# Expert 7's first layer cut into parts of 12, 2 and 2 blocks, TensorE's rounds of two blocks, and w2 of expert 6 in one load

## The chip, the cores and the metric

The kernel runs on one core of a Trainium2 chip. The metric is the device time of that core in microseconds (us). Before the change three runs gave 180.59, 180.69 and 180.82 us; the median is 180.69 us.

## What is computed

Eight experts, each a two-layer perceptron on its own 256 tokens:

```python
# x (8, 256, 512), w1 (8, 512, 2048), w2 (8, 2048, 512), b1 (8, 2048), b2 (8, 512), all float32
h = np.matmul(x, w1) + b1[:, np.newaxis, :]
h = np.maximum(h, 0)
return (np.matmul(h, w2) + b2[:, np.newaxis, :]).astype(np.float32)
```

The weights are read as float32 (4 MB each of w1 and w2 per expert, 64 MB in all) and converted to float16 while they are loaded, so that 2 MB per matrix arrive on the chip. The output is 4 MB of float32.

## The kernel before

Names: E = 8 experts, T = 256 tokens, `nJ` = 16 blocks of 128 hidden columns, `LAG` = 3, `NW` = 3 buffers each for w1 and w2, `NPH` = 4 banks of PSUM for first-layer results, `QJ` = 8 blocks, `nQ` = 2 halves of a second layer. In the text, l1(e) and l2(e) are the first and second layer of expert e, and w1(e), w2(e) the loads of its weights.

**TensorE** (`run_tensor`) runs one loop over the steps 0 to 10, written as a loop of the engine (`Fori`), not unrolled. Step s does l1(s), if s < 8, and then l2(s - 3), if s >= 3. l1 is an inner loop of four rounds of four blocks (L278); a block is four matmuls (L288) into one bank of `ph`. Every two blocks it waits on `ph_free` until ScalarE has emptied earlier banks (L282). Ahead of each pair of matmuls stands an instruction that computes their addresses (`ahead`, L262). l2 first puts the bias into `po` with two matmuls (L303); then an inner loop of two halves (L311), each of which waits on `w2_in` (L313) and runs 16 matmuls (L318). `po` has two buffers, used by even and odd experts. At the end of a second layer TensorE waits until the other buffer of `po` has been emptied (L336, L337), and for `ph_free` to reach a count that says that a whole further expert's hidden blocks are there (L338). Steps 8 to 10 hold only l2(5), l2(6) and l2(7).

**ScalarE** (`run_scalar`) takes blocks in order: bias, ReLU and conversion of each block of l1 from `ph` into `hT` (`relu`, L106), sixteen in a step, and after them the copy of that step's finished second layer from `po` (`evict`, L118). For experts 6 and 7 VectorE copies one half and ScalarE the other.

**VectorE** (`run_vector`) transposes x of experts 2 to 7 (L222) and makes its halves of the last two copies.

**GpSimd** (`run_gpsimd`) issues the weight loads on one queue, in a fixed order: w1(e) waits until l1(e - 3) is finished (L162), w2(e) until l2(e - 3) is finished (L167), since each takes over that expert's buffer. `CUT` splits w2(6) into two loads of 8 blocks and w2(7) into two of 11 and 5 blocks, each with a semaphore of its own. Once the first part of w2(7) has landed, GpSimd issues the stores of the outputs of experts 4 and 5 (1024 KB) and of experts 0 to 3 (2048 KB) (L183 to L188).

**SyncE** (`run_sync`) waits for each load in turn and passes the news on to TensorE as a count (L145 for w1, L151 for w2, two counts for each w2). After the first part of w2(7) it waits for the copy of expert 6 and stores that expert's output (512 KB, L155); after the loop it stores expert 7's (512 KB, L389). These two stores go on SyncE's own DMA queue.

At the start x of experts 0 and 1 is transposed by TensorE through the identity (L372), into the banks `ph[2]` and `ph[3]`, and ScalarE copies each result into `xT` (L373); then all engines meet, and the order written out by hand begins.

Of the kernel before, what the change touches and what calls it, by code (L numbers as in the profile page):

```python
# [10 lines left out]
def kernel(  # L11
# [22 lines left out]
    NW = 3  # L34
    NX = 4
    NH = LAG + 1
    NPH = 4

    GROUPS = {0: 4, 4: 2}
    GROUP_OF = {f + i: (f, n) for f, n in GROUPS.items() for i in range(n)}  # L40
    FIRST = {0: 1, 1: 1, 2: 2, 4: 4}
    X_OF = {f + i: (f, n, i) for f, n in FIRST.items() for i in range(n)}
    CUT = {E - 2: nJ // 2, E - 1: 11 * nJ // 16}
    nQ = 2
    QJ = nJ // nQ
    ENDS = nTB * nQ
# [1 line left out]
    def sb(name, shape, dt=fp16):  # L48
# [15 lines left out]
    steps = hT[:, NH - 1, 0 : B * B // T, :].rearrange("p a (n c) -> p (a n) c", c=B)  # L64
    steps_turned = hT[:, NH - 1, B * B // T : 2 * B * B // T, :].rearrange(
        "p a (n c) -> p (a n) c", c=B)
    ph = [nc.alloc_psum_tensor(f"ph{i}", [P, 512], fp32).ap() for i in range(NPH)]
    po = nc.alloc_psum_tensor("po", [P, 2, nTB, 512], fp32).ap()

    def sem(name):  # L70
# [10 lines left out]
    ph_full = sem("ph_full")  # L81
    ph_free = sem("ph_free")
# [74 lines left out]
    def run_gpsimd():  # L157
        g = nc.gpsimd

        def load_w1(e):  # L160
            if e >= NW:
                g.wait_ge(ph_full, nJ * (e - NW + 1))  # L162
            g.dma_start(out=w1_sb[:, e % NW], in_=w1_of(e)).then_inc(s_w1[e % NW], 16)  # L163

        def load_w2(e):
            if e >= NW:
                g.wait_ge(po_full, ENDS * (e - NW + 1))  # L167
            src = w2[e].rearrange("(p j) h -> p j h", j=nJ)
            cuts = (0, CUT[e], nJ) if e in CUT else (0, nJ)
            for h, (lo, hi) in enumerate(zip(cuts, cuts[1:])):  # L170
                g.dma_start(  # L171
                    out=w2_sb[:, e % NW, lo:hi], in_=src[:, lo:hi]).then_inc(s_w2[e, h], 16)

        for step in range(1, E + LAG):
            if step < E:
                if step == 4:
                    g.dma_start(out=x16[step], in_=x_of(step)).then_inc(s_x, 16)
                load_w1(step)
            if step == NW - 1:
                tc.wait_critical_data_deps()  # L180
            if step >= LAG:
                load_w2(step - LAG)
        g.wait_ge(s_w2[E - 1, 0], 16)  # L183
        for first in sorted(GROUPS, reverse=True):
            done = 1 + first + GROUPS[first]
            g.wait_ge(po_free_a, done)
            g.dma_start(out=out_of(first, GROUPS[first]), in_=grouped[first]).then_inc(  # L187
                s_out[first], 16)  # L188
    def run_scalar():
        a = nc.scalar  # L190
        a.sem_inc(ph_free, NPH)
        a.sem_inc(po_free_a, 1)
        a.sem_inc(po_free_d, 1 + len(GROUP_OF))
        a.sem_inc(xT_full, 2)  # L194
        a.copy(out=x16[2], in_=x32[2]).then_inc(cast, 1)  # L195
        for step in range(E + LAG):
            if step < E:
                for j in range(nJ):
                    a.wait_ge(ph_full, nJ * step + j + 1)
                    relu(step, j).then_inc(ph_free, 1)  # L200
# [36 lines left out]

    def run_tensor():
        t = nc.tensor
        mult, mod, least = (getattr(mybir.AluOpType, n) for n in ("mult", "python_mod", "min"))  # L240
# [4 lines left out]
        names = ("due", "w1_at", "x_at", "due2", "w2_at", "h_at", "o_at", "b_at", "next_e", "all_h", "next_s")  # L245
        due, w1_at, x_at, due2, w2_at, h_at, o_at, b_at, next_e, all_h, next_s = (
            t.alloc_register(n) for n in names)
        t.reg_mov(x_at, 0)
        for r in (w1_at, due2, w2_at, h_at, o_at, b_at, next_e):
            t.reg_add(r, x_at, 0)  # L250
        t.reg_add(due, x_at, 2)
        t.reg_add(next_s, x_at, 1)

        def val(r, top, low=0):
            return t.snap(r, min_val=low, max_val=top)

        def turn_over(r, by, size):
            t.reg_add(r, r, by)
            t.reg_alu(r, r, size, mod)
# [6 lines left out]
                "p (q j) -> p q j", j=nJ)[:, :, 0]  # L266

        with t.Fori(0, E + LAG) as s:
            with t.If(s < E):
                turn = val(next_s, E, 1)  # L270
                t.wait_ge(w1_in, turn)
                t.wait_ge(xT_full, turn)
                t.reg_add(next_s, next_s, 1)
                x_e = val(x_at, (NX - 1) * nKC * T)
                x_cols = [xT_f[:, bass.ds(x_e + kc * T, T)] for kc in range(nKC)]
                ahead(*x_cols[0:2])
                ahead(*x_cols[2:4])
                with t.Fori(0, nJ // NPH):  # L278
                    w1_j = val(w1_at, (NW - 1) * nKC * M + nJ - NPH)
                    for i in range(NPH):  # L280
                        if i % 2 == 0:
                            t.wait_ge(ph_free, val(due, E * nJ, 1))  # L282
                        for kc in range(nKC):
                            if kc % 2 == 0:
                                ahead(w1_cols(w1_j, i, kc), w1_cols(w1_j, i, kc + 1), weights=True)
                            if i % 2 == 1 and kc == nKC - 1:
                                t.reg_add(due, due, 2)
                            ins = t.matmul(  # L288
                                out=ph[i][:, 0:T],
                                lhsT=w1_cols(w1_j, i, kc),  # L290
                                rhs=x_cols[kc],
                                start=(kc == 0),
                                stop=(kc == nKC - 1),
                            )
                        ins.then_inc(ph_full, 1)
                    t.reg_add(w1_at, w1_at, NPH)
                turn_over(w1_at, nKC * M - nJ, NW * nKC * M)
                turn_over(x_at, nKC * T, NX * nKC * T)
            with t.If(s >= LAG):
                o = val(o_at, nTB * 512)  # L300
                b_e = val(b_at, (E - 1) * H)
                for tb in range(nTB):
                    t.matmul(  # L303
                        out=po_f[:, bass.ds(o + tb * 512, H)],
                        lhsT=ones1,
                        rhs=b2_sb[0:1, bass.ds(b_e, H)],
                        start=True,
                        stop=False,
                        skip_group_check=True,
                    )  # L310
                with t.Fori(0, nQ):  # L311
                    t.reg_add(due2, due2, 1)
                    t.wait_ge(w2_in, val(due2, nQ * E, 1))  # L313
                    w_e = val(w2_at, (NW * nJ - QJ) * H)
                    h_e = val(h_at, (NH * nJ - QJ) * T)
                    for tb in range(nTB):
                        for j in range(QJ):
                            ins = t.matmul(  # L318
                                out=po_f[:, bass.ds(o + tb * 512, H)],
                                lhsT=hT_f[:, bass.ds(h_e + (j * T + tb * P), P)],  # L320
                                rhs=w2_f[:, bass.ds(w_e + j * H, H)],
                                start=False,
                                stop=(j == QJ - 1),
                                skip_group_check=True,
                            )
                        ins.then_inc(po_full, 1)
                    turn_over(w2_at, QJ * H, NW * nJ * H)
                    turn_over(h_at, QJ * T, NH * nJ * T)
                turn_over(o_at, nTB * 512, 2 * nTB * 512)
                t.reg_add(b_at, b_at, H)  # L330
                t.reg_add(next_e, next_e, 1)
                t.reg_alu(all_h, next_e, nJ, mult)
                t.reg_add(all_h, all_h, nJ + NPH)
                t.reg_alu(all_h, all_h, E * nJ + NPH, least)
                done, turned = val(next_e, E, 1), val(all_h, E * nJ + NPH, 1)
                t.wait_ge(po_free_a, done)  # L336
                t.wait_ge(po_free_d, done)  # L337
                t.wait_ge(ph_free, turned)  # L338

    def first_loads():  # L340
        for to, rows in (
# [85 lines left out]
```

## Time and profile before

| what | value |
|---|---|
| median of three runs | 180.69 us |
| the profiled execution | 180.67 us, of which the span of the trace is 178.9 us |
| TensorE matmuls busy | 130.8 us (73%) |
| ScalarE busy | 86.2 us (48%) |
| VectorE busy | 37.7 us (21%) |
| moved by DMA | 40.98 MB at a mean of 229 GB/s, counted at the destination |
| read from memory / written to it | 71.39 MB / 4.19 MB |
| GpSimd's DMA queue (q0), SyncE's (q1) | 95.2% and 4.5% of 16 engines' span |

Times in the trace count from the start of the span. A row of the timeline gives the start, the length, the engine, the line, the operation and how many instructions were merged; in brackets stands the idle time before it and what ended that. "Landing" is the time from the issue of a transfer until its semaphore says that all of it has arrived. GpSimd's queue hands transfers to the 16 DMA engines in the order of issue. The share of DMA time over a short window can read above 1 because a packet is counted where it starts or overlaps.

### The profile page before, as it was taken

The page shows a single profiled execution, that of the slowest core. Times are in us where ns is not written, and L with a number is a line of the kernel's source. Part 1 is how long each engine was busy: PE and PEld are TensorE (multiplying, and loading weights), DVE is VectorE, ACT ScalarE, POOL GpSimd, SP SyncE. Part 2 cuts the span into 40 slices and gives each one's busy share as a digit, 9 for nine tenths or more (in the row PEclk, how much of TensorE's full clock was granted, in tenths as well). Part 3 has the DMA queues.
Part 4 walks back from the last instruction along what each step waited for, and adds up shares of the span by engine and source line. Part 5 has one row for each costly group of instructions (what it writes and reads, how often), then busy time and mean ns, then how long its engine had stood idle before and what let it go on. Part 6 is the DMA issues. An engine that isn't in the chain of part 4 may idle for free.

```text
span 178.9 us, 2880 instructions
## 1 busy us (share of the span) xinstructions
PE 130.8 (73%) x800; PEld 87.1 (49%) x800; DVE 37.7 (21%) x39; ACT 86.2 (48%) x160; POOL 13.4 (7%) x30
## 2 busy tenths in 40 slices
PE   0002299596969996999949993899389997997950
PEld 0002178585858742794338642764178543442410
DVE  0074099500000299992000000000000000001010
ACT  3302847585877803892099408970578303131010
POOL 7100000302020001001000001000200002000200
PEclk9999999999999999699999999999969999999995
DMA  5999989999999999998999999999899899999996
GB/s 215 265 255 277 233 183 231 234 205 207 234 209 202 234 212 198 234 231 183 231 234 201 209 234 205 205 234 220 191 234 231 187 227 205 214 213 212 335 440 256
DMA packets 3825, 40.98 MB, mean 229 GB/s; under 512 B 448, under 2 KB 464, under 8 KB 1136
## 3 DMA queue, kind: packets, MB, share of 16 engines
q0 software_dynamic: 3056, 37.76, 95.2%
q1 hardware_dynamic: 768, 3.21, 4.5%
q14 instruction: 1, 0.01, 0.0%
HBM read 71.39 MB, written 4.19 MB: 422 GB/s over the span
## 4 chain that ended last, share of the span: by engine, by line
DMA 62%; PE 20%; DVE 6%; ACT 4%; issue 3%; SPq 1%; ACTq 0%
DMA w1sb<-in_w_dram 43%; PE ph L288 12%; DMA outg<-in_x_dram 10%; DMA w2sb<-in_w_dram 10%; PE po L318 8%; DVE xTsb L222 6%; ACT hTsb L106 3%; ACT x L195 1%; SPq L347 1%; PE po L303 0%; ACT pair L118 0%; ACTq L422 0%; SPq L145 0%; SPq L151 0%; ACTq L194 0%
## 5 line engine op out<-in xcount | busy, mean ns | idle before, releaser
L288 PE MATMUL ph<-xTsb,w1sb 128*128 x512 | 68.1, 293 | 21.7 <-SPq L145 10.4
L288 PEld LDWEIGHTS ph<-xTsb,w1sb 128*128 x512 | 59.0, 148 | 31.9 <-issue 29.0
L106 ACT ACTIVATE hTsb<-ph,b1T 128x256 f16<-128x256 f32 x128 | 56.8, 474 | 15.4 <-PE ph L288 14.9
L318 PE MATMUL po<-w2sb,hTsb 128*128 x256 | 56.6, 379 | 2.3 <-SPq L151 2.3
L118 ACT COPY outg<-po 32x1024 f32<-32x1024 f32 (+1 forms) x20 | 20.1, 1005 | 43.3 <-PE po L318 43.2
L318 PEld LDWEIGHTS po<-w2sb,hTsb 128*128 x256 | 25.0, 98 | 32.8 <-issue 5.0
L222 DVE STREAM_TRANSPOSE xTsb<-x 32x512 f16<-32x512 f16 (+1 forms) x32 | 31.0, 970 | 35.0 <-DMA x<-in_x_dram 27.7
L118 DVE COPY pair<-po 128x512 f32<-128x512 f32 x2 | 1.4, 691 | 88.4 <-PE po L318 88.4
L372 PE MATMUL ph<-ident,x 128*128 128x128 f16 x16 | 1.9, 313 | 16.6 <-ACT ident L363 16.6
L171 POOL DMA_DIRECT2D w2sb<-in_w_dram x10 | 5.3, 534 | 70.7 <-PE po L318 70.7
L372 PEld LDWEIGHTS <-x 128*128 128x128 f16 x16 | 1.6, 148 | 16.6 <-ACT ident L363 16.6
L163 POOL DMA_DIRECT2D w1sb<-in_w_dram x7 | 3.7, 535 | 64.6 <-PE ph L288 64.4
L118 ACT COPY pair<-po 128x512 f32<-128x512 f32 x2 | 1.2, 585 | 13.8 <-PE po L318 13.8
L375 DVE STREAM_TRANSPOSE b1T<-b1rows 32x512 f32<-32x512 f32 x4 | 4.1, 1023 | 10.2 <-DMA b1rows<-in_b_dram 10.1
L303 PE MATMUL po<-b2sb,ones 1*128 x16 | 4.8, 379 | 0.9 <-issue 0.7
L363 ACT COPY ident<-hTsb 32x32 f16<-32x32 f16 x4 | 1.0, 240 | 9.2 <-DVE hTsb L360 9.1
L365 ACT CAST x<-pair 128x1024 f16<-128x1024 f32 x2 | 2.1, 1044 | 2.3 <-DMA pair<-in_x_dram 2.3
L303 PEld LDWEIGHTS po<-b2sb,ones 1*128 1x128 f16 x16 | 1.4, 91 | 3.5 <-issue 3.3
L373 ACT COPY xTsb<-ph 128x1024 f16<-128x1024 f16 x2 | 1.9, 1015 | 1.1 <-PE ph L372 1.1
L187 POOL DMA_DIRECT2D out_dram<-outg x2 | 1.1, 536 | 16.7 <-DMA w2sb<-in_w_dram 16.7
L195 ACT CAST x<-outg 128x2048 f16<-128x2048 f32 x1 | 1.9, 1900 | 0.8 <-DMA outg<-in_x_dram 0.8
L365 ACT ACT_TABLE_LOAD x1 | 1.3, 1283 | 0.7 <-PEq L411 0.7
(12 smaller groups left out, 5.0 us busy)
## 6 DMA issues: line engine op xcount, KB each, us to landing
w1sb<-in_w_dram POOLq DMA_DIRECT2D x8, 2048.0 KB, 30.6
w2sb<-in_w_dram POOLq DMA_DIRECT2D x6, 2048.0 KB, 43.8
w2sb<-in_w_dram POOLq DMA_DIRECT2D x2, 1024.0 KB, 28.4
out_dram<-outg POOLq DMA_DIRECT2D x1, 2048.0 KB, 10.9
w2sb<-in_w_dram POOLq DMA_DIRECT2D x1, 1408.0 KB, 17.5
pair<-in_x_dram SPq DMA_DIRECT2D x2, 512.0 KB, 3.8
outg<-in_x_dram SPq DMA_DIRECT2D x1, 1024.0 KB, 17.8
x<-in_x_dram POOLq DMA_DIRECT2D x1, 1024.0 KB, 27.7
```

The costliest lines, as they stand in the source:

```text
L106: return nc.scalar.activation(out=to, in_=columns, func=relu_of, bias=b1T[:, at : at + 1], scale=1.0)
L118: return copy(out=t.rearrange("p (tb s) h -> p tb s h", s=split)[at : at + rows, lo:hi, k, :], in_=po[k * rows : (k + 1) * rows, e % 2, lo ...
L163: g.dma_start(out=w1_sb[:, e % NW], in_=w1_of(e)).then_inc(s_w1[e % NW], 16)
L171: g.dma_start(out=w2_sb[:, e % NW, lo:hi], in_=src[:, lo:hi]).then_inc(s_w2[e, h], 16)
L195: a.copy(out=x16[2], in_=x32[2]).then_inc(cast, 1)
L222: ins = v.transpose(out=to[b * B : (b + 1) * B, :, :, half * B : (half + 1) * B], in_=src.rearrange("p r (i kc) -> p kc r i", kc=nKC))
L288: ins = t.matmul(out=ph[i][:, 0:T], lhsT=w1_cols(w1_j, i, kc), rhs=x_cols[kc], start=(kc == 0), stop=(kc == nKC - 1),)
L303: t.matmul(out=po_f[:, bass.ds(o + tb * 512, H)], lhsT=ones1, rhs=b2_sb[0:1, bass.ds(b_e, H)], start=True, stop=False, skip_group_check=True,)
L318: ins = t.matmul(out=po_f[:, bass.ds(o + tb * 512, H)], lhsT=hT_f[:, bass.ds(h_e + (j * T + tb * P), P)], rhs=w2_f[:, bass.ds(w_e + j * H, ...
L365: a.copy(out=x16[e], in_=x32[e])
L372: t.transpose(out=to[:, kc, r, :], in_=rows[:, kc, :], identity=ident)
L375: v.transpose(out=b1T[b * B : (b + 1) * B, nB - 1 - b : nB - 1 - b + nJ * B], in_=b1_rows.rearrange("r (i j) -> r j i", j=nJ))
```

## The change

- l1(7) is cut. `LAST = (6, 1, 1)` gives its rounds in steps 7, 8 and 9: 12 blocks ahead of l2(4), 2 blocks between l2(4) and l2(5), and 2 blocks between l2(5) and l2(6). The number of rounds left out of a step is held in a packed register (`skipped`) from which each step takes three bits as the first index of its inner loop.
- A round of l1 has two blocks in place of four, for all experts. The bank of `ph` is now computed from a register (`p_at`), so the four banks are one tensor `ph_all`. For expert 7 the pointers into w1 and x are not turned over between the parts.
- ScalarE takes 12 blocks of expert 7 in step 7, and the other 4 in step 8, ahead of the copy of expert 5.
- The wait for hidden blocks at the end of a second layer (L338) goes, with the three register operations that computed its count.
- w2(6) is one load of 2048 KB with one semaphore in place of two of 1024 KB.

```diff
+    ROUNDS = nJ // 2
+    LAST = (6, 1, 1)
+    SKIPPED = [0] * (E - 1) + [ROUNDS - n for n in LAST]
...
-    CUT = {E - 2: nJ // 2, E - 1: 11 * nJ // 16}
+    CUT = {E - 1: 11 * nJ // 16}
...
-    ph = [nc.alloc_psum_tensor(f"ph{i}", [P, 512], fp32).ap() for i in range(NPH)]
+    ph_all = nc.alloc_psum_tensor("ph", [P, NPH, 512], fp32).ap()
+    ph = [ph_all[:, i] for i in range(NPH)]
...
+    def columns_at(step):
+
+        if step < E - 1:
+            return range(nJ)
+        return {E - 1: range(2 * LAST[0]), E: range(2 * LAST[0], nJ)}.get(step, ())
+
     def run_scalar():
...
         for step in range(E + LAG):
-            if step < E:
-                for j in range(nJ):
-                    a.wait_ge(ph_full, nJ * step + j + 1)
-                    relu(step, j).then_inc(ph_free, 1)
+            for j in columns_at(step):
+                e = min(step, E - 1)
+                a.wait_ge(ph_full, nJ * e + j + 1)
+                relu(e, j).then_inc(ph_free, 1)
...
+        t.reg_add(skipped, x_at, sum(n << 3 * step for step, n in enumerate(SKIPPED)))
...
         with t.Fori(0, E + LAG) as s:
-            with t.If(s < E):
+            with t.If(s < len(SKIPPED)):
                 turn = val(next_s, E, 1)
                 t.wait_ge(w1_in, turn)
                 t.wait_ge(xT_full, turn)
-                t.reg_add(next_s, next_s, 1)
+                t.reg_alu(first, skipped, 7, and_)
+                t.reg_alu(skipped, skipped, 3, right)
...
-                with t.Fori(0, nJ // NPH):
-                    w1_j = val(w1_at, (NW - 1) * nKC * M + nJ - NPH)
-                    for i in range(NPH):
-                        if i % 2 == 0:
-                            t.wait_ge(ph_free, val(due, E * nJ, 1))
+                with t.Fori(val(first, 7), ROUNDS):
+                    w1_j = val(w1_at, (NW - 1) * nKC * M + nJ - 2)
+                    p = val(p_at, (NPH - 2) * 512)
+                    t.wait_ge(ph_free, val(due, E * nJ, 1))
+                    for i in range(2):
...
-                                out=ph[i][:, 0:T],
+                                out=ph_f[:, bass.ds(p + i * 512, T)],
...
-                    t.reg_add(w1_at, w1_at, NPH)
-                turn_over(w1_at, nKC * M - nJ, NW * nKC * M)
-                turn_over(x_at, nKC * T, NX * nKC * T)
+                    t.reg_add(w1_at, w1_at, 2)
+                    turn_over(p_at, 2 * 512, NPH * 512)
+                with t.If(s < E - 1):
+                    t.reg_add(next_s, next_s, 1)
+                    turn_over(w1_at, nKC * M - nJ, NW * nKC * M)
+                    turn_over(x_at, nKC * T, NX * nKC * T)
...
-                t.reg_alu(all_h, next_e, nJ, mult)
-                t.reg_add(all_h, all_h, nJ + NPH)
-                t.reg_alu(all_h, all_h, E * nJ + NPH, least)
-                done, turned = val(next_e, E, 1), val(all_h, E * nJ + NPH, 1)
+                done = val(next_e, E, 1)
                 t.wait_ge(po_free_a, done)
                 t.wait_ge(po_free_d, done)
-                t.wait_ge(ph_free, turned)
```

More of the change, by code (lines that the diff above doesn't have):

```diff
@@ L239, in run_tensor @@
         t = nc.tensor
-        mult, mod, least = (getattr(mybir.AluOpType, n) for n in ("mult", "python_mod", "min"))
+        mod, and_, right = (getattr(mybir.AluOpType, n) for n in (
+            "python_mod", "bitwise_and", "logical_shift_right"))
         xT_f = xT.rearrange("p n kc t -> p (n kc t)")
@@ L244, in run_tensor @@
         po_f = po.rearrange("p n tb h -> p (n tb h)")
-        names = ("due", "w1_at", "x_at", "due2", "w2_at", "h_at", "o_at", "b_at", "next_e", "all_h", "next_s")
-        due, w1_at, x_at, due2, w2_at, h_at, o_at, b_at, next_e, all_h, next_s = (
+        ph_f = ph_all.rearrange("p n c -> p (n c)")
+        names = ("due", "w1_at", "x_at", "due2", "w2_at", "h_at", "o_at", "b_at", "next_e", "next_s",
+                 "skipped", "first", "p_at")
+        due, w1_at, x_at, due2, w2_at, h_at, o_at, b_at, next_e, next_s, skipped, first, p_at = (
             t.alloc_register(n) for n in names)
         t.reg_mov(x_at, 0)
-        for r in (w1_at, due2, w2_at, h_at, o_at, b_at, next_e):
+        for r in (w1_at, due2, w2_at, h_at, o_at, b_at, next_e, p_at):
             t.reg_add(r, x_at, 0)
@@ L285, in run_tensor @@
                                 ahead(w1_cols(w1_j, i, kc), w1_cols(w1_j, i, kc + 1), weights=True)
-                            if i % 2 == 1 and kc == nKC - 1:
+                            if i == 1 and kc == nKC - 1:
                                 t.reg_add(due, due, 2)
                             ins = t.matmul(
-                                out=ph[i][:, 0:T],
+                                out=ph_f[:, bass.ds(p + i * 512, T)],
                                 lhsT=w1_cols(w1_j, i, kc),
```

## The prediction

> **What bounds the kernel now.** I read the page's shares of engines and queues first.
>
> ```profile
> PE 130.8 (73%) x800; PEld 87.1 (49%) x800; DVE 37.7 (21%) x39; ACT 86.2 (48%) x160; POOL 13.4 (7%) x30
> ...
> q0 software_dynamic: 3056, 37.76, 95.2%
> q1 hardware_dynamic: 768, 3.21, 4.5%
> ```
>
> The two queues add up to 99.7% of the DMA engines' time. No engine comes near this. Next the landings of the last weight loads, each asked for by itself: w2(4), w2(5), and the two parts each of w2(6) and w2(7).
>
> ```profile
> L171 POOL DMA_DIRECT2D w2sb<-in_w_dram x1: 527/527/527, 89.3 to 89.3; - x1
> DMA to landing us min/median/max: 49.6/49.6/49.6
> ...
> L171 POOL DMA_DIRECT2D w2sb<-in_w_dram x1: 527/527/527, 108.3 to 108.3; - x1
> DMA to landing us min/median/max: 40.3/40.3/40.3
> ...
> L171 POOL DMA_DIRECT2D w2sb<-in_w_dram x2: 527/531/535, 127.3 to 127.8; - x2
> DMA to landing us min/median/max: 26.3/28.4/30.6
> ...
> L171 POOL DMA_DIRECT2D w2sb<-in_w_dram x2: 527/532/538, 147.6 to 148.1; - x2
> DMA to landing us min/median/max: 17.5/18.7/20.0
> ```
>
> Issue plus landing: w2(4) is there at 138.9, w2(5) at 148.6, w2(6) at 153.6 and 158.4, 11 of 16 blocks of w2(7) at 165.1 and the rest at 168.1. Each 2 MB takes 9.7 us behind the one before (148.6 - 138.9), and 11/16 of 9.7 is 6.7, just the 165.1 - 158.4 that is seen. So the loads run end to end; a transfer waits in the queue, not for its issue. TensorE's last stretch shows the same from the other side:
>
> ```profile
> 130.15 9.39 PE L288 MATMUL ph<-xTsb,w1sb 128*128 x64 [3.15 <-SPq L145]
> ...
> 140.22 7.08 PE L318 MATMUL po<-w2sb,hTsb 128*128 x32
> ...
> 148.83 7.08 PE L318 MATMUL po<-w2sb,hTsb 128*128 x32 [1.00 <-SPq L151]
> 155.84 0.60 PE L303 MATMUL po<-b2sb,ones 1*128 x2
> 156.38 7.08 PE L318 MATMUL po<-w2sb,hTsb 128*128 x32
> ...
> 165.24 7.08 PE L318 MATMUL po<-w2sb,hTsb 128*128 x32 [1.25 <-SPq L151]
> ```
>
> l2(5) and l2(7) wait for their weights (0.2 us after the landing); l2(6) began at 156.38, with one half of w2(6) there and the other to come at 158.4, before its second half needed it. Last the tail: the final store, and what the two queues did in two windows, 173.3 to 176 and 176 to 178.
>
> ```profile
> L389 SPq DMA_DIRECT2D out_dram<-pair x1: 344/344/344, 173.3 to 173.3; - x1
> ...
> DMA to landing us min/median/max: 4.7/4.7/4.7
> ```
> ```profile
> q0 software_dynamic: 67, 1.06, 92.0%
> q1 hardware_dynamic: 2, 0.01, 0.7%
> ```
> ```profile
> q1 hardware_dynamic: 142, 0.52, 63.1%
> ```
>
> The rows of the queues give packets, MB and the share of the 16 engines' time. The last store (q1, 512 KB) is issued at 173.3, but the DMA engines work on q0's stores until 176 and on the last store only then. The end too belongs to the DMA engines, not to the instruction that issues the store.
>
> **The parts of the change.**
>
> *w2(6) in one load.* It removes one transfer from the stream. Two halves took 158.4 - 148.6 = 9.8 us against 9.7 for whole loads; both are rounded to 0.1, so the gain lies between 0 and 0.2. I take 0.05: **-0.05**. The price: l2(6) can no longer begin on half of its weights. They are there at 158.4 - 0.05, so its L318 starts 0.2 later, at 158.55, in place of 156.38. From the start of one second layer to the next with nothing to wait for it is 156.38 - 148.83 = 7.55, so l2(7) starts at 166.1 in place of 165.24: 0.86 later, and with it the copy and the last store's issue, near 174.2.
>
> *What hides that 0.86.* At the start of the kernel a 512 KB transfer on q1, with idle engines, shows what the last one would take alone:
>
> ```profile
> L347 SPq DMA_DIRECT2D pair<-in_x_dram x2: 387/404/422, 0.7 to 1.2; - x2
> ...
> DMA to landing us min/median/max: 3.4/6.3/17.8
> ```
>
> 3.4 us against 4.7: the last store now stands 1.3 us behind q0's stores. Issued up to 1.3 us later it finds the engines free just then, and nothing is lost; beyond that each us costs a us. So 0.86 costs **0** (ends: 0 and 0.86, if 512 KB stored takes the full 4.7 by itself; the row of a free queue is nearer to a queue that has just emptied). The store of expert 6 (L155) is moved too: it waits for the copy after l2(6), so it goes from 165.2 to some 166.4, behind GpSimd's two stores, in the rows below. It is the same half MB for the same engines, so their work ends no later. SyncE's next wait, for the second part of w2(7) (168.1), lies after that, and l2(7) needs its count at 166.1 + 3.5.
>
> ```profile
> 155.95 2.02 ACT L118 COPY outg<-po 64x1024 f32<-64x1024 f32 x2 [6.59 <-PE po L318]
> ...
> 165.20 0.34 SPq L155 DMA_DIRECT2D out_dram<-pair  x1
> ...
> 165.33 1.06 POOL L187 DMA_DIRECT2D out_dram<-outg  x2 [16.68 <-DMA w2sb<-in_w_dram]
> ```
>
> *The parts of l1(7).* l2(4) starts when w2(4) is there (138.9 + 0.2 = 139.1) or when 12 blocks are done: four blocks less (64 matmuls in 8.09 below, so 0.51 a block) than 139.54, plus 0.68 to the first L318, gives 138.2. So 139.1, and its end at 146.2; w2(7) is issued some 1.1 us earlier, which buys nothing, since it lies behind w2(6) until 158.4. Then two blocks: 0.83 us from count to first matmul, 1.01 us of work, 0.68 to the next L318, 2.5 in all: 148.7, against 148.83 where l2(5) starts anyway. The same after l2(5): 155.9 + 2.5 = 158.4, against 158.55. Both parts **just fit, by 0.15 us**. The entry is the uncertain term. It is 0.83 after a wait (the chain of waits, first fence) and 1.73 between two first layers with nothing to wait for (second fence, 42.34 to 44.07); between two second layers, as above, it is hidden altogether.
>
> ```profile
> 129.32 0.02 SPq L145
> 129.34 0.81 issue
> 130.15 6.03 PE ph L288 x36
> ```
> ```profile
> 34.25 8.09 PE L288 MATMUL ph<-xTsb,w1sb 128*128 x64 [1.79 <-DVE xTsb L222]
> 36.28 1.73 PEld L288 LDWEIGHTS ph<-xTsb,w1sb 128*128 x16 [0.31 <-issue]
> 44.07 8.14 PE L288 MATMUL ph<-xTsb,w1sb 128*128 x64 [1.73 <-issue]
> ```
>
> With 1.73 a part takes 3.4: l2(5) at 149.6, l2(6) at 160.1, l2(7) at 167.6, 2.4 late, and 2.4 - 1.3 = 1.1 on the time. I take 0.83, because the end of a second layer hides the way to the next one now. Ends: **0 and +1.1**.
>
> *ScalarE's order.* Blocks 12 to 15 ahead of the copy of expert 5 delay that copy (2.02 us in the row above) from 155.95 to after 158.3, so it ends near 160.4. Its PSUM buffer is needed by l2(7) at 166.1 and its output by GpSimd's stores at 165.3: over 4 us of cover, 0. The removed wait on `ph_free` never ended an idle time in the rows above: 0.
>
> *Rounds of two.* Four more loop turns in each l1. In the rows above weight loads pause 0.31 us at a turn, matmuls less than 0.1: between 0 and 1.2 us per l1. In the middle it delays only issues of loads that land 26 to 50 us later (the second fence): 0. It counts in l1(0), with the next part.
>
> *One tensor for four banks.* At the start the transposes of expert 1 write into the tensor that ScalarE is still reading for expert 0, and the order written for TensorE has a wait there now.
>
> ```profile
> 2.12 17.78 DMA outg<-in_x_dram
> ```
> ```profile
> 16.63 1.90 PE L372 MATMUL ph<-ident,x 128*128 128x128 f16 x16 [16.63 <-ACT ident L363]
> 17.71 1.93 ACT L373 COPY xTsb<-ph 128x1024 f16<-128x1024 f16 x2 [1.14 <-PE ph L372]
> 22.05 10.40 PE L288 MATMUL ph<-xTsb,w1sb 128*128 x64 [3.52 <-issue]
> 32.75 0.53 POOL L163 DMA_DIRECT2D w1sb<-in_w_dram x1 [27.69 <-PE ph L288]
> ```
>
> Half of the transposes (0.95) then run after the first copy (17.71 + 0.97), and the second copy (0.97) ends at 20.7 in place of 19.64. All engines meet after that; now they wait for x until 19.90 (the first row, from the chain of waits), so l1(0) starts 0.9 later. With 0 to 1.2 for its turns (half of it cold and slow, so I take 0.4), w1(3) is issued 1.3 us later (0.9 to 2.1). What covers that is what still lies in the queue:
>
> ```profile
> L163 POOL DMA_DIRECT2D w1sb<-in_w_dram x1: 530/530/530, 32.8 to 32.8; - x1
> ...
> DMA to landing us min/median/max: 14.2/14.2/14.2
> ```
>
> Alone, 2 MB would take 9.7 plus what 512 KB takes beside its data: 3.4 less 1.3 (512 KB at the 1.06 MB in 2.7 us of q0's window above), 2.1. So of 14.2 some 2.4 us are waiting. 1.3 < 2.4: **0**, ends 0 and about +0.5 if a load's own start is a little longer. [...]
>
> **Sum.** -0.05 on the profiled 180.67 gives 180.62; the median of the runs is 0.02 above that execution, so **180.65 us**. Times within 0.2% (0.36 us) are about what measurement can tell from no change.
>
> **Rivals.**
>
> *TensorE becomes the bound at the end* (slower). Place: the entry into the two short parts. If it costs over 1.17 us each (l2(7) starts at 146.2 + 7.08 + 7.55 + twice 1.69 and twice the entry), l2(7) starts over 1.3 us late and the last store is no longer covered. For it: 1.73 in the row at 44.07. Against it: 0 between two second layers. Time: up to 180.6 + 1.1 = 181.7; half-way 181.2.
>
> *The queue runs dry at the start* (slower). Place: w1(3), due in the queue near 35. It decides once l1(0) ends over 2.4 us later; the whole stream shifts by what is beyond. For it: a delay of up to 2.1 with a cover known to some tenths. Time 180.9 to 181.3.
>
> *The earlier issue of w2(7) moves its landing* (faster). If its landing hung on the issue, 1.1 us would be gained: 179.6. Against it: it lands 6.7 us after w2(6), the pure transfer time.
>
> *A transfer less saves its fixed part* (faster). The two halves of w2(6) land as fast as one load, 9.8 against 9.7 us; if instead each carried a start of 2.1 us, as worked out above, that much would go: 178.6. [...] The spacing in this trace does not show it, since in a full queue the next transfer flows meanwhile.
>
> **How the numbers follow.** No measurable change 0.57; TensorE at the end 0.22; the dry queue 0.13; the two faster ones 0.04 each. Faster 0.08, same 0.57, slower 0.35. The range runs from 180.4 (a gain of 0.2 at the merged load) to 181.6 (nearly the full 1.1 at the end); it leaves out the faster rivals and a slower case in which both delays add up. The likeliest case by itself spans 180.4 to 180.9.
>
> **What the profile after would show.** The first part of w2(7) landing near 165.0, L318 of l2(6) starting near 158.6 and of l2(7) near 166.1, the last store issued near 174.1 and landing in 3.4 to 4.0 us, w1(3) issued near 34 and landing some 12.9 us later. The prediction is wrong if w1(3) lands after 47.0, or if l2(7) starts after 166.6.

## The result and the profile after

The changed kernel takes 203.88 us (median of six runs, 203.36 to 204.93) against 180.75 us for the kernel before on the same chips: a ratio of 1.128, 95% interval 1.125 to 1.131. It is 12.8% slower, where no measurable change was forecast and the range ended at 181.6. The profiled execution took 203.93 us, its span is 202.1 us. (The kernel with parts and rounds of four, below, ran in two groups of times: three runs at 181.6 to 181.8 us with a granted clock of 0.99 to 1.00, and five at 185.6 to 188.3 us with 0.95 to 0.96, where the kernel before had 0.96 to 0.98 beside it; its ratio is that of the first group, its profile one of the second.)

What bounds the kernel is another engine now. The shares of the chain of work that ended last, of before and of after:

```profile
DMA 62%; PE 20%; DVE 6%; ACT 4%; issue 3%; SPq 1%; ACTq 0%
```
```profile
PE 52%; ACT 18%; DMA 16%; issue 10%; POOL 2%; SPq 0%; POOLq 0%
```

GpSimd's queue falls from 95.2% to 85.3% of the span, and the hole is near the end. From the page of after, GB/s in 40 slices of 5.05 us, and GpSimd's queue:

```profile
GB/s 256 220 258 263 211 208 233 178 208 212 214 211 240 214 208 211 214 227 227 211 208 214 214 224 227 211 208 217 211 94 156 208 52 0 181 214 88 444 214 104
...
q0 software_dynamic: 2912, 37.76, 85.3%
```

Through the first 29 slices (146 us) the rate stays at 178 or more; after them come slices of 94, 52 and 0. The loads of w2(5), w2(6) and w2(7) show why:

```profile
L175 POOL DMA_DIRECT2D w2sb<-in_w_dram x1: 528/528/528, 129.8 to 129.8; - x1
DMA to landing us min/median/max: 21.0/21.0/21.0
...
L175 POOL DMA_DIRECT2D w2sb<-in_w_dram x1: 527/527/527, 151.8 to 151.8; - x1
DMA to landing us min/median/max: 12.4/12.4/12.4
...
L175 POOL DMA_DIRECT2D w2sb<-in_w_dram x2: 527/532/537, 170.7 to 171.2; - x2
DMA to landing us min/median/max: 9.6/10.8/12.1
```

Their issues were at 108.3, 127.3 and 147.6; now they come 21.5, 24.5 and 23.1 us later. In the slice around the issue of w2(7), from 166.7 to 171.7, nothing moves: its first part, 11 of 16 blocks, lands after 9.6 us in a queue that was empty. So the loads are issued late, because GpSimd waits for the end of a second layer (idle 21.5, 21.5 and 18.4 us ahead of these three until L336), and from l1(2) on TensorE never waits for a load. Its rows of one step of after (l1(4), l2(1)):

```profile
86.21 1.12 PE L303 MATMUL ph<-xTsb,w1sb 128*128 x8 [0.73 <-issue]
87.74 1.11 PE L303 MATMUL ph<-xTsb,w1sb 128*128 x8 [0.41 <-issue]
90.71 1.09 PE L303 MATMUL ph<-xTsb,w1sb 128*128 x8 [1.85 <-ACT hTsb L110]
92.21 1.09 PE L303 MATMUL ph<-xTsb,w1sb 128*128 x8 [0.41 <-ACT hTsb L110]
...
100.40 7.08 PE L336 MATMUL po<-w2sb,hTsb 128*128 x32
```

A round of two blocks takes 1.50 to 1.53 us from start to start: 1.09 of matmuls and 0.41 in which TensorE stands still. Before, 16 blocks took 8.09, so two blocks took 1.01. With eight rounds and seven such pauses a first layer takes 11.7 us in place of 8.1, and that moves everything. Rows of before, then of after, in order of time:

```profile
53.92 8.10 PE L288 MATMUL ph<-xTsb,w1sb 128*128 x64 [1.71 <-issue]
...
62.73 7.08 PE L318 MATMUL po<-w2sb,hTsb 128*128 x32
72.00 9.23 PE L288 MATMUL ph<-xTsb,w1sb 128*128 x64 [2.19 <-SPq L145]
...
119.92 7.08 PE L318 MATMUL po<-w2sb,hTsb 128*128 x32
```
```profile
78.40 7.08 PE L336 MATMUL po<-w2sb,hTsb 128*128 x32
...
144.39 7.08 PE L336 MATMUL po<-w2sb,hTsb 128*128 x32
...
163.29 7.08 PE L336 MATMUL po<-w2sb,hTsb 128*128 x32
171.04 1.12 PE L303 MATMUL ph<-xTsb,w1sb 128*128 x8 [0.67 <-issue]
...
173.14 7.08 PE L336 MATMUL po<-w2sb,hTsb 128*128 x32
...
190.53 7.08 PE L336 MATMUL po<-w2sb,hTsb 128*128 x32
```

The whole loss can be read off these second layers:

| stretch | before | after | more |
|---|---|---|---|
| up to the start of l2(0) (four first layers) | 62.73 | 78.40 | 15.67 |
| l2(0) to l2(3) (three steps) | 57.19 | 65.99 | 8.80 |
| l2(3) to l2(7) | 45.32 | 46.14 | 0.82 |
| landing of the last store | 4.7 | 2.6 | -2.1 |
| sum | | | 23.2 |

The times of the two profiled executions differ by 203.93 - 180.67 = 23.26. Two thirds of the loss arise before the first second layer.

### The profile page after: what moved, and what is told of

The parts are those of the page before. It is cut to its first block, busy times and chain, and to the rows that moved or that the text cites. A ratio compares the mean times of both kernels' runs of the same rounds, so it can differ in the third digit from the quotient of the medians.

```text
span 202.1 us, 3094 instructions
## 1 busy us (share of the span) xinstructions
PE 140.1 (69%) x800; PEld 88.4 (44%) x800; DVE 37.8 (19%) x39; ACT 87.2 (43%) x160; POOL 12.9 (6%) x29
## 3 DMA queue, kind: packets, MB, share of 16 engines
q0 software_dynamic: 2912, 37.76, 85.3%
## 4 chain that ended last, share of the span: by engine, by line
PE 52%; ACT 18%; DMA 16%; issue 10%; POOL 2%; SPq 0%; POOLq 0%
PE po L336 28%; PE ph L303 22%; DMA w1sb<-in_w_dram 16%; ACT hTsb L110 9%; ACT outg L122 8%; PE po L321 2%; POOL hTsb L370 0%; POOL w1sb L366 0%; ACT pair L122 0%; POOL w1sb L167 0%; POOL b2sb L366 0%; POOL ones L372 0%; POOL hTsb L373 0%; POOL ident L371 0%; SPq L149 0%
## 5 line engine op out<-in xcount | busy, mean ns | idle before, releaser
L303 PE MATMUL ph<-xTsb,w1sb 128*128 x512 | 77.2, 305 | 36.5 <-ACT hTsb L110 19.8
L303 PEld LDWEIGHTS ph<-xTsb,w1sb 128*128 x512 | 60.5, 150 | 54.8 <-issue 50.3
L110 ACT ACTIVATE hTsb<-ph,b1T 128x256 f16<-128x256 f32 x128 | 57.6, 475 | 45.3 <-PE ph L303 44.9
L336 PE MATMUL po<-w2sb,hTsb 128*128 x256 | 56.6, 379 | 0.0
L336 PEld LDWEIGHTS po<-w2sb,hTsb 128*128 x256 | 24.9, 98 | 30.4 <-issue 2.6
L175 POOL DMA_DIRECT2D w2sb<-in_w_dram x9 | 4.8, 534 | 76.5 <-PE po L336 76.5
```

The costliest lines, as they stand in the source:

```text
L110: return nc.scalar.activation(out=to, in_=columns, func=relu_of, bias=b1T[:, at : at + 1], scale=1.0)
L175: g.dma_start(out=w2_sb[:, e % NW, lo:hi], in_=src[:, lo:hi]).then_inc(s_w2[e, h], 16)
L303: ins = t.matmul(out=ph_f[:, bass.ds(p + i * 512, T)], lhsT=w1_cols(w1_j, i, kc), rhs=x_cols[kc], start=(kc == 0), stop=(kc == nKC - 1),)
L336: ins = t.matmul(out=po_f[:, bass.ds(o + tb * 512, H)], lhsT=hT_f[:, bass.ds(h_e + (j * T + tb * P), P)], rhs=w2_f[:, bass.ds(w_e + j * H, ...
```

## The experiments

**Which part of the change it is.** The rounds of two alone, in the kernel before (banks as one tensor, since the bank is taken from a register; no parts, w2(6) in two loads):

```diff
-                with t.Fori(0, nJ // NPH):
-                    w1_j = val(w1_at, (NW - 1) * nKC * M + nJ - NPH)
-                    for i in range(NPH):
+                with t.Fori(0, nJ // 2):
+                    w1_j = val(w1_at, (NW - 1) * nKC * M + nJ - 2)
+                    p = val(p_at, (NPH - 2) * 512)
+                    for i in range(2):
...
-                                out=ph[i][:, 0:T],
+                                out=ph_f[:, bass.ds(p + i * 512, T)],
...
+                    turn_over(p_at, 2 * 512, NPH * 512)
```

> The kernel before with rounds of two blocks and a bank from a register, and nothing else of the change: 16 blocks of expert 7 in one step, w2(6) in two loads. Theory (the round of two by itself makes TensorE's instruction stream the bound, about 1.52 us a round and 12 us a first layer): l2(4) starts near 166, l2(7) near 189, time 201 to 203.5 us. Rival (the parts and the single load of w2(6) make the end late): 181 to 186 us, with l2(4) starting before 145.

Measured 199.70 us, ratio 1.105 (1.103 to 1.108), a little under the range expected: 19 of the 23 us. And the complement, the change with its parts and its one load of w2(6), but with rounds of four fixed banks (the short parts as blocks of their own under conditions):

```diff
-    SKIPPED = [0] * (E - 1) + [ROUNDS - n for n in LAST]
+    SKIPPED = [0] * (E - 1) + [1, 4, 4]
...
+                with t.If(s < E):
+                    with t.Fori(val(first, 7), nJ // NPH):
+                        blocks(0, NPH, val(w1_at, top - NPH))
+                with t.If(s >= E):
+                    with t.If(s < E + 1):
+                        blocks(0, 2, val(w1_at, top - 2))
+                    with t.If(s >= E + 1):
+                        blocks(2, 4, val(w1_at, top - 2))
```

> The changed kernel, parts of 12, 2 and 2 blocks and w2(6) in one load, but with the rounds of four and the four fixed banks of before; only the two short parts stand apart as blocks of their own. Theory (rounds alone): the first layers take 8.1 us again, l2(6) starts near 158.6 and l2(7) near 166.1, time 180.4 to 181.1 us; the end and the single load are neutral, as predicted. Rival (parts and load cost): above 185 us.

Ratio 1.0051 (1.0031 to 1.0070): +0.9 us, where at most 0.4 was expected. So the rounds of two carry most of it: 19 of the 23 us by themselves. What the parts and the one load cost without them is taken up below, with a kernel in which ScalarE copies less. In the profiled execution of this one (185.94 us) TensorE waits after each second layer for ScalarE's copy, and what follows runs slowly (timeline, then windows of TensorE's granted clock, the third number from the end):

```profile
93.70 1.97 PE L300 MATMUL ph<-xTsb,w1sb 128*128 x16 [0.71 <-issue]
98.11 7.15 PE L300 MATMUL ph<-xTsb,w1sb 128*128 x48 [2.44 <-ACT hTsb L109]
```
```profile
98.10:105.30 7.20, 7.15 (x48) 6.17 (x48) 0.00 (x0) 5.59 (x14) 0.00 (x0) 0.76 1.03 218
```

48 matmuls take 7.15 us at a granted clock of 0.76, against 6.07 in the undisturbed stretch of before (94.15) at 1.00. A wait of 2.44 us stands ahead of that stretch.

**What the 0.41 us are.** The rows name ScalarE as the releaser. If that were so, a shorter ReLU would shorten the round. So ScalarE does half of each block, and the other half is left out:

```diff
+        to, columns = hT[:, e % NH, j, 0 : T // 2], ph[j % NPH][:, 0 : T // 2]
...
-                                lhsT=hT_f[:, bass.ds(h_e + (j * T + tb * P), P)],
+                                lhsT=hT_f[:, bass.ds(h_e + j * T, P)],
```

> The changed kernel, but ScalarE applies bias and ReLU to 128 of the 256 columns of each block, and the second layers read those 128 for both halves of the tokens: half of the hidden activations are left out. Theory (the 0.41 us before each round is TensorE's own instruction stream): rounds stay at 1.50 to 1.53 us, the 0.41 us gap stays, time 202 to 204 us. Rival (the gap is a wait on ScalarE, as the profile puts it): ScalarE's two blocks take about 0.3 us less, the gap falls below 0.15 us and the time below 195 us.

199.67 us (one run), between the two forecasts. The rounds did not shorten:

```profile
94.31 1.09 PE L304 MATMUL ph<-xTsb,w1sb 128*128 x8 [0.42 <-ACT hTsb L111]
...
150.10 1.91 PE L304 MATMUL ph<-xTsb,w1sb 128*128 x16
...
161.91 7.08 PE L337 MATMUL po<-w2sb,hTsb 128*128 x32
...
170.33 7.08 PE L337 MATMUL po<-w2sb,hTsb 128*128 x32
```

ScalarE falls as the cause: two blocks of it took 0.80 us instead of 0.91, a smaller cut than the 0.3 us expected, and none of it arrived, since the pause stayed 0.42. Most of the 4.2 us that this kernel saves come from a side effect. Its second layer reads the same columns for both halves of the tokens, so its half-loop has 10 address instructions in the compiled program in place of 18, and behind it the gaps are gone: two rounds run through in 1.91 us (150.10), and a part costs 8.42 us from one second layer to the next (161.91 to 170.33) where after has 9.85 (163.29 to 173.14), 2.9 us for the two parts. Fewer address instructions ahead of the matmuls, no gap behind them: this pointed at TensorE's own instruction stream. The next kernel replaces the sum and remainder that turn the bank over by a bitwise operation:

```diff
-                    turn_over(p_at, 2 * 512, NPH * 512)
+                    t.reg_alu(p_at, p_at, 2 * 512, mybir.AluOpType.bitwise_xor)
```

> The changed kernel with the bank register flipped by one exclusive-or in place of an addition and a remainder. Theory (the number of instructions and the loop turn cost, not the remainder): 1.48 to 1.52 us a round, time 201 to 204 us. Rival (the remainder is slow on the sequencer): a round falls by 0.2 us or more, a first layer by 1.6 us or more, time below 195 us.

212.21 us (one run), slower still, against 201 to 204 expected. The compiler could no longer fold the operation into the instruction that computes addresses: in place of one of those, three plain register instructions stand in the round, two more in all. Rounds go from 1.51 to 1.64 us:

```profile
72.78 1.09 PE L303 MATMUL ph<-xTsb,w1sb 128*128 x8 [0.39 <-ACT hTsb L110]
74.42 1.09 PE L303 MATMUL ph<-xTsb,w1sb 128*128 x8 [0.55 <-ACT hTsb L110]
```

That is a dose. So doses were given to the kernel before, in its rounds of four: address instructions that nobody uses, n = 2 and n = 8 of them at the end of each round.

```diff
+                    for n in range(2):
+                        ahead(*(w1_f[:, bass.ds(w1_j + (64 + 32 * n + 16 * h), 16)] for h in range(2)))
                     t.reg_add(w1_at, w1_at, NPH)
```

> The kernel before, rounds of four static banks, with two more register instructions (an address computed and not used) at the end of each round, nothing else. Theory (TensorE's own instruction stream is what is full): a round of four is as full as its 1.97 + 0.08 us of matmuls, so two instructions at about 0.06 us each show as a longer wait between rounds, 0.12 to 0.25 us, first layer 8.5 to 9.0 instead of 8.1; the step of about 19.0 us of TensorE's own work becomes 19.4 to 19.9, at or over DMA's 19.4: 180.7 to 183. Rival (register instructions run beside matmuls at no cost, and it is the branch of the turn that costs): first layer 8.1, 180.7. Rival (slack of 2 us and more per step, as the prediction had it): 180.7 whatever the first layer becomes.

> The same with eight more register instructions per round of four. Theory: 0.5 to 0.8 us a round, first layer 10.0 to 11.3, TensorE's step 21 to 22 us, over DMA's 19.4, w2 of 5 to 7 issued later and the queue dry after 160: 188 to 197 us. Rival (instructions cost nothing beside matmuls): 180.7. Rival (the turn's branch): 180.7.

Then the bank from a register without more turns, which is four more address instructions per round of four, spread over its blocks:

```diff
-                                out=ph[i][:, 0:T],
+                                out=ph_f[:, bass.ds(p + i * 512, T)],
...
+                    turn_over(p_at, NPH * 512, NPH * 512)
```

> The kernel before with the PSUM bank of the first layer's output taken from a register, in rounds of four (four more register instructions per round of four, one for each block, and the same number of turns and branches as before). Theory: as any four instructions, 0.25 to 0.5 us a round, first layer 9.0 to 10.0, 182 to 188 us. If the turn of the loop is what costs, not the instructions: 180.7 with a first layer of 8.1. If a matmul whose bank comes from a register is itself slower: matmuls of the round no longer 0.123 us apart, whatever the waits between rounds.

And a jump more in each round, with no other instruction:

```diff
+                    blocks(range(2))
+                    with t.If(s < E + LAG):
+                        blocks(range(2, 4))
```

> The kernel before with the last two blocks of each round under a condition that is always true, which leaves one more jump in TensorE's instructions per round of four and no other instruction. Eight turns instead of four put half a jump more on each two blocks; the rest of the 0.50 us that a round of two costs over half a round of four would be the three more register instructions. At the 0.125 us that each register instruction cost in rounds of four, three make 0.37 and leave 0.13 for half a turn, so a turn's jump costs 0.2 to 0.3: rounds 2.25 to 2.35 apart instead of 2.05, first layer 8.9 to 9.3, 182.5 to 186 us. If a jump costs no more than another instruction: rounds 2.17 apart, first layer 8.6, 181 to 182.5. If a jump costs nothing: 180.7.

The times of the first three of these kernels, in the table below, all came out above the range expected, because an instruction had been put at as little as 0.06 us, a term that no run shows; the runs showed 0.12 to 0.14. Rounds with two, eight and four instructions more, in this order:

```profile
101.23 1.96 PE L288 MATMUL ph<-xTsb,w1sb 128*128 x16 [0.32 <-ACT hTsb L106]
103.56 1.97 PE L288 MATMUL ph<-xTsb,w1sb 128*128 x16 [0.36 <-ACT hTsb L106]
```
```profile
68.32 1.97 PE L288 MATMUL ph<-xTsb,w1sb 128*128 x16 [1.16 <-ACT hTsb L106]
71.46 1.97 PE L288 MATMUL ph<-xTsb,w1sb 128*128 x16 [1.18 <-ACT hTsb L106]
```
```profile
65.62 2.17 PE L291 MATMUL ph<-xTsb,w1sb 128*128 x16 [0.30 <-ACT hTsb L107]
68.23 2.13 PE L291 MATMUL ph<-xTsb,w1sb 128*128 x16 [0.43 <-ACT hTsb L107]
```

Four blocks are counted from the start of a round to the start of the next, as the mean of the rounds that neither a wait nor a lower clock stretches (with the banks by register they range from 2.48 to 2.61):

| kernel | address instructions more per four blocks | four blocks, us | more per instruction | start of l2(0) | time, us | ratio (interval) |
|---|---|---|---|---|---|---|
| before | 0 | 2.05 | | 62.73 | 180.8 | |
| one jump more | 0 | 2.05 | | 60.74 | 180.91 | 1.0003 (0.9986 to 1.0021) |
| two more | 2 | 2.31 | 0.13 | 66.97 | 183.56 | 1.012 (1.008 to 1.016) |
| banks by register | 4 | 2.54 | 0.12 | 71.24 | 190.70 | 1.054 (1.051 to 1.058) |
| eight more | 8 | 3.14 | 0.14 | 78.35 | 203.90 | 1.128 (1.123 to 1.132) |
| the change | 6, and a turn | 3.03 | 0.16 with the turn | 78.40 | 203.88 | 1.128 (1.125 to 1.131) |

Each address instruction cost 0.12 to 0.14 us, 0.13 already at a dose of two: nothing of that was hidden beside the matmuls, so the stream of before was already full. Eight of them bring the kernel before to the time of the change, with its static banks and its four turns. Where they stood mattered little (0.12 each spread over the blocks, 0.13 and 0.14 at the end of the round); spread over the blocks they also stretched the matmuls (2.13 to 2.17 against 1.97). The compiled change has 16 address instructions per four blocks where before has 10; six at 0.12 to 0.14 are 0.72 to 0.84 of the 0.98 that four blocks take longer, and 0.14 to 0.26 is left for the one turn more, or somewhat more than that, since the change's rounds have one plain register instruction less. That turn was not measured by itself. The jump more cost nothing that can be seen, against 182.5 to 186 expected: a miss. It is not the jump of a turn either. The compiler settled the condition, which is always true, and left a jump without a comparison to the instruction right behind it, while a turn compares and goes back. (Its l2(0) starts 2 us early because l1(0) did, not because its rounds are shorter.)

The trace has a meter for it, the idle time of the weight loads that nothing releases. Rows of before, of eight more, of after (busy time and mean, then the idle time and its part by "issue"):

```profile
L288 PEld LDWEIGHTS ph<-xTsb,w1sb 128*128 x512 | 59.0, 148 | 31.9 <-issue 29.0
```
```profile
L288 PEld LDWEIGHTS ph<-xTsb,w1sb 128*128 x512 | 60.5, 149 | 53.4 <-issue 49.3
```
```profile
L303 PEld LDWEIGHTS ph<-xTsb,w1sb 128*128 x512 | 60.5, 150 | 54.8 <-issue 50.3
```

**The step and the other parts.** w2(6) in one load, alone (`CUT = {E - 1: 11 * nJ // 16}`):

> The kernel before with w2 of expert 6 in one load and nothing else; rounds of four, no parts. If the load is worth what the prediction gave it (0.05 us earlier landing of the last parts, second layer of 6 starting 2.2 us later at 158.55 and of 7 at 166.1, all of it covered by the wait for the last parts and by the last store's queue): 180.65 us, within 0.2 of the kernel before. If the delay of the second layer of 6 is not covered: 181.3 to 181.6, with the last second layer's start 0.9 later and the last store issued 0.9 later. If a fixed cost of one load less is saved: 180.2 or less, and w2 of 7 lands 0.3 us earlier.

180.82 us against 180.81, ratio 1.0008 (0.9985 to 1.0031), with the rows that were forecast:

```profile
158.66 7.08 PE L318 MATMUL po<-w2sb,hTsb 128*128 x32 [0.46 <-SPq L151]
...
166.22 7.08 PE L318 MATMUL po<-w2sb,hTsb 128*128 x32
```

The banks as one tensor, alone (`ph = [ph_all[:, i] for i in range(NPH)]`):

> The kernel before with its four PSUM banks as one tensor, rounds of four with fixed banks, nothing else. The prediction's step: the second transposes wait for ScalarE's first copy, about 1 us, first layer of 0 0.9 later, all covered: 180.7 within 0.3. If TensorE's slack of 0.4 us a step decides at the start as well: 181.2 to 181.8.

180.72 us, ratio 0.9987 (0.9975 to 0.9999): it costs nothing that can be seen. The second half of the transposes waits, as forecast:

```profile
15.90 1.04 PE L373 MATMUL ph<-ident,x 128*128 128x128 f16 x8 [15.90 <-ACT ident L364]
18.05 1.01 PE L373 MATMUL ph<-ident,x 128*128 128x128 f16 x8 [1.10 <-ACT xTsb L374]
```

Next the wait of 1.85 us in each step of after. ScalarE copies a second layer's results before it goes on with the next first layer (timeline of after):

```profile
85.52 4.07 ACT L122 COPY outg<-po 32x1024 f32<-32x1024 f32 x4 [7.65 <-PE po L336]
89.61 1.57 ACT L110 ACTIVATE hTsb<-ph,b1T 128x256 f16<-128x256 f32 x4
```

VectorE takes over half of every copy, first with rounds of four, then in the change itself:

```diff
     def scalar_from(e):
-        return 0 if e in GROUP_OF else nTB // 2
+        return nTB // 2
```

> The changed kernel with rounds of four static banks (the same parts of 12, 2 and 2 blocks, w2 of 6 in one load), and with VectorE copying half of every expert's outputs, not only those of 6 and 7, so that ScalarE is 2 us shorter after each second layer. Theory (a step of TensorE is second layer, first round, the wait for ScalarE's copy, three rounds; what exceeds DMA's 19.4 us is paid): the wait of 2.4 us after the first round shrinks to under 0.8, TensorE's step to 17.5 to 18.8 us, under DMA's 19.4, the loads land as before the change and the parts cost nothing: 180.4 to 181.3, last second layer at 165 to 166.5. If the parts themselves cost (the branches at the end, or the first layer's last blocks coming between second layers): 182 to 186 with the last second layer at 168 or later and the wait on ScalarE gone all the same.

> The change itself, rounds of two, with VectorE copying half of every expert's outputs. Theory: the wait of 1.85 us for ScalarE's copy in each step goes nearly whole, the step of 22.0 becomes 20.1 to 20.5, still over DMA's 19.4: 187 to 195 us. If ScalarE's copy is not part of the step (the rounds of two wait for something else in its place): 201 to 204.

With rounds of four: 181.67 us, ratio 1.0049 (1.0031 to 1.0067), between the two forecasts. The wait on ScalarE after the first round is gone, and a load holds TensorE up again in the middle: l1(6) starts at 112 us, 1.1 us after its load landed (110.9):

```profile
111.99 8.15 PE L301 MATMUL ph<-xTsb,w1sb 128*128 x64 [1.89 <-issue]
...
140.15 7.08 PE L343 MATMUL po<-w2sb,hTsb 128*128 x32 [0.31 <-SPq L154]
148.23 1.09 PE L301 MATMUL ph<-xTsb,w1sb 128*128 x8 [1.00 <-issue]
...
150.28 7.08 PE L343 MATMUL po<-w2sb,hTsb 128*128 x32
158.62 1.10 PE L301 MATMUL ph<-xTsb,w1sb 128*128 x8 [1.27 <-issue]
```

From l2(4) to l2(7) nothing but TensorE's own order is left, and l2(7) starts at 167.92, 2.7 us later than before. But not all of this is the parts. The merged load alone makes it 1.0 (166.22, above), and the loads themselves are late, from w1(2) on. Landings of w1(1) and w1(2), the least and the greatest of two, before and in this kernel, and a queue that this kernel's page has and that of before has not:

```profile
L163 POOL DMA_DIRECT2D w1sb<-in_w_dram x2: 535/546/557, 4.0 to 4.5; - x2
DMA to landing us min/median/max: 23.6/28.1/32.7
...
L166 POOL DMA_DIRECT2D w1sb<-in_w_dram x2: 535/547/559, 4.0 to 4.5; - x2
DMA to landing us min/median/max: 23.6/28.7/33.7
...
q8 instruction: 1, 0.02, 0.0%
```

w1(2) landed 1.0 us later after its issue, and the loads behind it stayed late: w2(6) landed at 159.35 instead of 158.41. l2(6) began 1.0 us after that landing, against 0.2 with the merged load alone, so the parts cost 0.8 us there. The time is 0.8 us longer, no more than the loads are late, and the last store gives back 1.6 of TensorE's delay (3.1 us to land in place of 4.7). So the cost of the parts in the end is not shown here. The late w1(2) (33.7 us from issue to landing, against 32.7 before and 33.0 in the change) and the fetch of instructions of 0.02 MB (q8) come together in this kernel, and before and the change have no q8; that the fetch makes the load late was not tested.

In the change itself the split gave 197.82 us, ratio 1.093 (1.090 to 1.097): six us less than the change. The step went from 22.0 to 20.5 us (l2(0) at 78.17, l2(3) at 139.77), as the theory said, but the sum expected, 187 to 195, was too low, because it left out what lies ahead of the first second layer: l2(0) still starts 15.4 us late.

## Why the prediction was wrong

**The step that failed is "Rounds of two".** It was wrong in both of its halves.

The size: "between 0 and 1.2 us per l1" was 3.6 us (11.7 against 8.1). The pause of 0.31 us in the weight loads at each turn was taken for the price of a turn, and the edit for four turns more. The doses speak for something else, a stream without any lead: the last instruction's work was done and the next was not there yet (the weight loads' idle time under "issue" was 29.0 us before, 34.8 with two instructions more a round, 37.8 with four, 49.3 with eight). Each added instruction cost 0.12 to 0.14 us, and the change adds 24 address instructions to each first layer (64 against 40): 24 at 0.12 to 0.14 are 2.9 to 3.4 of the 3.6. The prediction counted turns, not instructions.

The cover: "In the middle it delays only issues of loads that land 26 to 50 us later". That cover belongs to the loads. TensorE's own work stands in a row, and it has a pace of its own. The four first layers at the start have no cover at all: between them TensorE waited for no load, as the row at 44.07 says, which the prediction itself quotes (1.73 us, "issue"). So l2(0) takes the full price of 15.67 us: three first layers 3.6 longer each, the first one, slow anyway, 1.3, its start 1.4 later, and 2.3 for longer ways from one layer to the next. Against that, before, l1(4) waited only 2.19 us for its load. After that a step of after takes 22.0 us, while two loads take 2 x 9.7 = 19.4. TensorE then sets the pace; the loads are issued ever later, and their 26 us of waiting in the queue are used up at w2(6). The doses show the same curve: two instructions a round cost 2.75 us in the end, four cost 9.9, eight 23.1, so little slack there was.

**w2(6) in one load: right**, by its own run: l2(6) at 158.66 (forecast 158.55), l2(7) at 166.22 (166.1), the last store landing in 3.9 us, time unchanged.

**One tensor: right.** Second transposes 1.10 us later, covered.

**The parts of l1(7): left open.** In the change a part with its way in and out costs 9.85 - 7.55 = 2.30 us, near the 2.5 forecast, with an entry of 0.67; but there the loads no longer set the end, so it is paid. With rounds of four, and with conditions around the parts, the entries are 1.00 and 1.27 us and l2(6) starts 0.8 us later than its load would let it. The time measured there, 181.67 us, is the upper time of the first rival, TensorE at the end (181.7). That is no proof of it: the loads were 1.0 us late before any part began, which no rival named. The cover at the end was also larger than the prediction took, since the last store alone lands in 2.6 us (after), not 3.4, so 2.1 us of its 4.7 were waiting, not 1.3. Whether the parts would fit with the entry of 0.67 and a first layer of 8 us was not tried.

**ScalarE's order: right for expert 5, but it was the wrong copy to look at.** The copies of experts 0 to 4 stand ahead of the next first layer's blocks, and once TensorE no longer waits for a load there, it waits for them: 1.85 us of each step.

**The other rivals.** The queue at the start: w1(3), issued at 35.4, landed 13.6 us later, at 49.0, past the 47.0 that the prediction named as a sign against it; but TensorE was by then later than its loads, and nothing waited for it. The queue ran dry at the end, for the reason above, which no rival named. The two faster rivals fell: the merged load saved nothing by itself, and with the banks as one tensor w2(7) was issued 0.7 us earlier than before (146.9) and landed no earlier (165.1).

## What to carry to other kernels

The loop of matmuls whose addresses come from registers was bound here by TensorE's instruction stream and not by its matmuls (after: 1.09 us of matmuls in a round of 1.50 to 1.53); idle time of the weight loads put down to "issue" at every turn was its sign (0.31 us at a turn before), and then each instruction added to the loop is to be counted; in these runs each address instruction was paid for with 0.12 to 0.14 us. Ask of every engine, not only of the one that bounds, how long its own work of one step is, and how far that is from the step of the bound. A releaser named in a row is the event that came last, not always the cause: a kernel in which that releaser is made shorter tells it (here ScalarE's two blocks went from 0.91 to 0.80 us and the pause stayed at 0.42). When a variant comes out slower by as much as a rival said, look at the landings before believing it.

## What the runs showed of the hardware

An instruction that computes matmul addresses in registers cost 0.12 to 0.14 us of TensorE's time (two, four and eight more of them in a round of four blocks); a plain register instruction less (with the bitwise operation three of them in place of one address instruction made a round 0.13 us longer, 1.64 in place of 1.51, so some 0.09 each, an estimate); a jump to the next instruction nothing that can be seen (four blocks 2.05 with and without it). With these prices little is left for the matmuls in the stream: (2.05 - 10 x 0.12) / 16, an estimate of at most 0.053 us each, if the stream takes one instruction after the other.

The last store of 512 KB landed in 2.6 us when nothing else was in the queues (after: issued at 198.6, every other transfer landed by 195.6), in 3.1 with rounds of four and the split (issued at 176.0), in 3.9 with the merged load alone (174.3), and in 4.7 in the kernel before (173.3), where GpSimd's store of 2 MB landed only at 176.8: what an earlier or a later issue was worth at the end depended here on what still stood in the other queue.
